# Copies for sums of weight blocks, paced by tiles of the stage that runs beside them, in a decoder block on one core

## The chip, the cores and the metric

The program runs on one core of a Trainium2 chip. The core has TensorE (PE, with its weight loads as PEld), VectorE (DVE), ScalarE (ACT), GpSimd (POOL) and SyncE (SP), which here only issues DMA transfers. The metric is the device time of one execution in microseconds (us), lower being better; the median of three runs counts.

## The reference

One layer of a decoder block on 1024 tokens of width 1024, all in float32:

```python
h = rms_norm(x, norm_mix)
q_flat, kv_flat, g_attn, u_pool, g_merge = split(h @ w_in)
a = nsa_attention(q_flat, kv_flat, g_attn, ...) @ w_branch_attn   # compressed, selected, window branches
b = pool_mixer(u_pool, pool_w, pool_scale) @ w_branch_pool        # trailing means over 2, 4, 8, 16 tokens
ga, gb = split(sigmoid(g_merge))
x = x + (ga * a + gb * b) @ w_out
h = rms_norm(x, norm_mlp)
x = x + square(relu(h @ w_ff1)) @ w_ff2                           # 1024 -> 4096 -> 1024
return rms_norm(x, norm_final)
```

## The kernel before, in words

Every product of float32 matrices is made of three matmuls (`mm3`, L74 to L79): each operand is split into a part rounded to the matmul's type and a rest, and high x high, high x low and low x high are added in PSUM. The split of a weight is made on the fly in `load` (L164 to L183): SP loads 128 x 512 values into `wraw` (four buffers), ScalarE casts them to `whi` (three buffers), and GpSimd, or VectorE where the call says so, subtracts to get `wlo` (three buffers).

The stages, in order of time. First the keys and values of the projection, with `x` loaded and normalised (0 to about 53 us). Then a second block of the projection with 280 columns together with the compression of keys and values (to about 140 us), and two blocks of queries, stored to DRAM as `qd` through two buffers `q` after a rotation on GpSimd (to about 265 us). Their weights stay resident in ten buffers `bhi` and `blo`. Then the pooling branch (`pool_in`, `pool_mix`, to about 345 us) and the gated projection, a loop over eight column blocks `m` of 128 (L480 to L501), which stores the tiles `gb` to DRAM as `gbd`. Then attention (to about 852 us): a written-out interleaving of 32 pairs of heads, 8 blocks of 128 queries by 4 pairs, each pair writing its part of `oT`; between their steps PE gets 128 terms of the other gate's projection, `ga_terms`, stored as `tad`. Then the merge of the branches and the output projection, in two halves of 512 tokens (`ta` and `gb` are loaded back, to about 1003 us), and the feed-forward part.

The feed-forward matrices are multiplied by a scheme of seven block products in place of eight, which needs sums of weight blocks. `weight_sums` (L198 to L216) makes these 32 sums in DRAM, each 1 MB: a copy of one block into `wsw_ff`, issued by SP, and later a DMA from POOL that adds a second block or an earlier sum onto it. The generator is advanced once per `m` of the gated projection and up to 26 times in the attention. Its copies have no input but the weights and write fresh DRAM. The program is scheduled by a framework that sets the order on each engine by its own estimate of when an instruction's inputs are there, so the order in the source isn't that on the engines.

Of the kernel before, what the change touches and what calls it, by code (L numbers as in the profile page):

```python
# [8 lines left out]
F32 = mybir.dt.float32  # L9
# [8 lines left out]
P = 128  # L18
S = 1024
# [3 lines left out]
HALF = 512  # L23
# [26 lines left out]
def build(tc, a, out, dbg=None):  # L50
    nc = tc.nc
# [141 lines left out]
    tad = [[dram.tile([P, HALF], F32, name=f"tad{m}_{h}") for h in range(2)] for m in range(NK)]  # L193


    wsum = {}

    def weight_sums():  # L198
        late = []
        for layer in ("w_ff1", "w_ff2"):  # L200
            for fh in range(2):
                for p in (7, 6, 5, 3):
                    for h in range(2):
                        d = dram.tile([P, 2048], F32, name=f"ws{layer}{fh}{p}{h}")
                        wsum[layer, fh, p, h] = d
                        (m0, k0), (m1, k1) = {7: ((0, 0), (1, 0)), 6: ((1, 1), (0, 0)), 5: ((1, 0), (1, 1)),
                                              3: ((0, 1), (0, 0))}[p]
                        nc.sync.dma_start(d, a[layer][fh, m0, k0, h])
                        prior = {6: 7, 3: 6}.get(p)
                        late.append((d, a[layer][fh, m1, k1, h] if prior is None else wsum[layer, fh, prior, h]))  # L210
                        if len(late) > 1:
                            d_, src = late.pop(0)
                            nc.gpsimd.dma_start(d_, src, accum_op=ADD, max_dma_last_dim=2048)
                        yield
        for d_, src in late:
            nc.gpsimd.dma_start(d_, src, accum_op=ADD, max_dma_last_dim=2048)  # L216

    sums = weight_sums()


# [201 lines left out]
    with ExitStack() as st:  # L422
# [6 lines left out]
        with ExitStack() as st2:  # L429
# [48 lines left out]
                    pool_mix(*prev)  # L478
                prev = cur
            for m in range(NK):  # L480
                next(sums)
                gh, gl = load(cols(a["w_in"], C_GB + m * P, P))
                bh, bl = load(cols(a["w_branch_pool"], m * P, P, 0, 4))
                zz = []
                for hf in range(2):
                    sl = slice(hf * HALF, (hf + 1) * HALF)
                    ps = psF.tile([P, HALF], F32, name="psF")
                    mm3(ps, [(gh[:, k], gl[:, k], XH[k][:, sl], XL[k][:, sl]) for k in range(NK)])
                    z = wg.tile([P, HALF], F32, name="z", bufs=3)
                    nc.vector.tensor_tensor(z, ps, rB[:, sl], op=MUL)  # L490
                    nc.scalar.activation(z, z, AF.Tanh, scale=0.5)
                    zz.append(z)
                if m == 0:
                    pool_mix(*prev)
                for hf in range(2):
                    sl = slice(hf * HALF, (hf + 1) * HALF)
                    ps = psF.tile([P, HALF], F32, name="psF")
                    mm3(ps, [(bh[:, k], bl[:, k], mxh[:, k, sl], mxl[:, k, sl]) for k in range(4)])
                    gb = wg.tile([P, HALF], F32, name="gb", bufs=2)
                    nc.vector.scalar_tensor_tensor(gb, zz[hf], 1.0, ps, op0=ADD, op1=MUL)  # L500
                    nc.sync.dma_start(gbd[m][hf], gb)  # L501


    octx = ExitStack()
    op = pool(octx, "o", side="right")
    oT = op.tile([P, 4, S], F32, name="oT")
    with ExitStack() as st:
# [172 lines left out]
        pairs = [(i, hp) for i in range(NT) for hp in range(NH // 2)]  # L680
        weight = [min(i + 1, 5) + i + 2 for i, _ in pairs]
        total, nterm = sum(weight), 2 * NK * NK
        done, given, summed = 0.0, 0, 0

        def advance(w):
            nonlocal done, given, summed
            done += w
            while summed < 26 * done / total:
                next(sums, None)
                summed += 1  # L690
            while given < nterm and given < nterm * done / total:
                next(fill, None)
                given += 1
# [5 lines left out]
        for n in range(len(pairs) + 1):  # L699
            aseq = []  # L700
            if n < len(pairs):
                i, hp = pairs[n]
# [14 lines left out]
            for fn, slot in bseq or [(None, True)]:  # L717
                if fn is not None:
                    fn()
                if slot:  # L720
# [3 lines left out]
                        ia += 1  # L724
                    advance(bw / nslot)
            assert ia == na
            if n < len(pairs):
                bseq, bw = units_b(u), weight[n]
        for _ in fill:
            pass  # L730
        for _ in sums:
            pass
        sctx.close()
        dump("oT", oT)
    psTctx.close()
# [44 lines left out]
    with ExitStack() as st:  # L780
        wm = pool(st, "wm")
        for hf in range(2):
# [7 lines left out]
            for m in range(NK):  # L790
                wh, wl = load(cols(a["w_branch_attn"], m * P, P, 0, 4), nc.vector)
                ps = bank()
                mm3(ps, [(wh[:, k], wl[:, k], oh[:, k], ol[:, k]) for k in range(4)])
                ta = wm.tile([P, HALF], F32, name="ta", bufs=2)
                gb = wm.tile([P, HALF], F32, name="gb", bufs=1)
                nc.sync.dma_start(ta, tad[m][hf])
                nc.sync.dma_start(gb, gbd[m][hf])
                nc.vector.scalar_tensor_tensor(ta, ta, 1.0, ps, op0=ADD, op1=MUL)
                nc.vector.tensor_tensor(ta, ta, gb, op=ADD)
                mh = wm.tile([P, HALF], F32R, name=f"mh{m}")  # L800
                ml = wm.tile([P, HALF], F32R, name=f"ml{m}")
                nc.scalar.copy(mh, ta)
                sub(nc.vector, ml, ta, mh)
                mg.append((mh, ml))
# [220 lines left out]
```

## Time and profile before

| | |
|---|---|
| median of 3 runs | 1652.23 us (1650.91 to 1655.87) |
| profiled execution | 1656.69 us |
| its span | 1654.9 us, mean granted TensorE clock 0.943 |
| PE busy | 1480.2 us, 89% of the span |
| DVE, ACT, POOL busy | 1001.7, 758.6, 169.1 us |
| moved by DMA | 204.67 MB, mean 124 GB/s |

A busy time is the time in which an engine executes something; issues of DMA transfers and waits aren't in it. The granted clock is a share of TensorE's full speed. The DMA share is the mean busy share of the core's 16 DMA engines as the packets show it, and can pass 1. A wait is put down to the engine or transfer that came last, by line: `POOL wsw_ff L213 <- DMA wsw_ff<-in_w_ff` says that GpSimd waited in front of its DMA at line 213 until a transfer into `wsw_ff` had landed.

### The profile page before, as it was taken

The page shows a single profiled execution, that of the slowest core. Times are in us where ns is not written, and L with a number is a line of the kernel's source. Part 1 is how long each engine was busy: PE and PEld are TensorE (multiplying, and loading weights), DVE is VectorE, ACT ScalarE, POOL GpSimd, SP SyncE. Part 2 cuts the span into 40 slices and gives each one's busy share as a digit, 9 for nine tenths or more (in the row PEclk, how much of TensorE's full clock was granted, in tenths as well). Part 3 has the DMA queues.
Part 4 walks back from the last instruction along what each step waited for, and adds up shares of the span by engine and source line. Part 5 has one row for each costly group of instructions (what it writes and reads, how often), then busy time and mean ns, then how long its engine had stood idle before and what let it go on. Part 6 is the DMA issues. An engine that isn't in the chain of part 4 may idle for free.

```text
span 1654.9 us, 20716 instructions
## 1 busy us (share of the span) xinstructions
PE 1480.2 (89%) x7369; PEld 1222.5 (74%) x7369; DVE 1001.7 (61%) x1928; ACT 758.6 (46%) x1561; POOL 169.1 (10%) x206
## 2 busy tenths in 40 slices
PE   8766554669999999999998989999999999999995
PEld 6755453558877788887876878888888888888874
DVE  5554101331118888887765575766789656669984
ACT  4332110121227877777753344557434453764441
POOL 2111333122220000000001010000000000001020
PEclk9878677789999999999999999999999999999997
DMA  8999999962231110010046533333333333333322
GB/s 304 289 286 222 262 275 280 230 144 83 77 102 46 38 46 21 33 33 26 27 136 214 148 104 107 94 100 97 97 95 97 96 96 96 96 96 97 96 63 102
DMA packets 130137, 204.67 MB, mean 124 GB/s; under 512 B 9840, under 2 KB 62832, under 8 KB 129520
## 3 DMA queue, kind: packets, MB, share of 16 engines
q1 hardware_dynamic: 112992, 169.78, 32.8%
q0 software_dynamic: 16896, 33.56, 11.5%
q8 instruction: 58, 0.95, 0.2%
q14 instruction: 47, 0.39, 0.1%
q10 hardware_dynamic: 144, 0.00, 0.0%
HBM read 186.52 MB, written 83.89 MB: 163 GB/s over the span
## 4 chain that ended last, share of the span: by engine, by line
PE 71%; DMA 3%; DVE 3%; ACT 2%; issue 1%; POOL 0%; POOLq 0%; DVEq 0%; SPq 0%; ACTq 0%
PE psm L79 14%; PE psm L77 14%; PE psm L78 14%; PE oacc L659 5%; PE psT L648 4%; PE psF L79 3%; PE psF L78 3%; PE psF L77 3%; DMA gb<-gbd 3%; PE psS L553 2%; PE psS L554 2%; PE psG L77 2%; PE psG L78 2%; PE psG L79 2%; PE psS L556 1%
## 5 line engine op out<-in xcount | busy, mean ns | idle before, releaser
L78 PE MATMUL psm<-mv,whi 128*128 128x512 f32 x896 | 351.9, 393 | 0.0
L77 PE MATMUL psm<-mv,whi 128*128 128x512 f32 x896 | 351.8, 393 | 0.0
L79 PE MATMUL psm<-mv,wlo 128*128 128x512 f32 x896 | 351.7, 393 | 0.0
L82 DVE TENSOR_TENSOR wlo<-wraw,whi 128x512 fp32r<-128x512 f32 x288 | 197.9, 691 | 109.9 <-ACT whi L858 70.3
L858 ACT CAST whi<-wraw 128x512 fp32r<-128x512 f32 x224 | 138.8, 620 | 247.9 <-PE psm L78 185.9
L78 PEld LDWEIGHTS psm<-mv,whi 128*128 128x128 f32 x896 | 169.0, 189 | 37.0
L77 PEld LDWEIGHTS psm<-mv,whi 128*128 128x128 f32 x896 | 168.9, 189 | 36.9
L79 PEld LDWEIGHTS psm<-mv,wlo 128*128 128x128 f32 x896 | 168.9, 188 | 36.8
L179 ACT CAST whi<-wraw 128x512 fp32r<-128x512 f32 x112 | 69.4, 622 | 175.3 <-PE psF L78 77.0
L79 PE MATMUL psF<-xh,wlo 128*128 128x512 f32 x192 | 79.1, 412 | 50.7 <-POOL wlo L82 50.7
L652 DVE TENSOR_TENSOR pl<-psT,ph 128x512 fp32r<-128x512 f32 (+1 forms) x160 | 101.9, 646 | 31.1 <-ACT ph L651 29.7
L754 POOL TENSOR_TENSOR sqa<-sqa,sq 128x512 f32<-128x512 f32 x24 | 33.1, 1381 | 803.0 <-ACT sq L750 803.0
L651 ACT CAST ph<-psT 128x512 fp32r<-128x512 f32 (+1 forms) x160 | 87.6, 555 | 50.1 <-PE psT L648 48.4
L563 DVE TENSOR_REDUCE nm<-psS 128x1 f32<-128x64 f32 (+8 forms) x192 | 99.6, 539 | 16.4 <-PE psS L556 9.0
L82 POOL TENSOR_TENSOR wlo<-wraw,whi 128x512 fp32r<-128x512 f32 x48 | 64.3, 1350 | 422.5 <-ACT whi L179 299.3
L77 PE MATMUL psF<-bhi,xh 128*128 128x256 f32 (+1 forms) x192 | 63.9, 335 | 40.0 <-ACT q L392 15.1
L79 PEld LDWEIGHTS psF<-xh,wlo 128*128 128x128 f32 x192 | 38.3, 199 | 60.2 <-POOL wlo L82 52.0
L77 PE MATMUL psF<-xh,whi 128*128 128x512 f32 x192 | 78.4, 408 | 2.8 <-ACT q L392 2.8
L78 PE MATMUL psF<-xl,whi 128*128 128x512 f32 x192 | 78.0, 406 | 0.0
L77 PEld LDWEIGHTS psF<-bhi,xh 128*128 128x128 f32 x192 | 43.9, 230 | 42.8 <-ACT q L392 15.4
L564 ACT ACTIVATE pS<-psS,nm 128x64 f32<-128x64 f32 (+8 forms) x128 | 67.9, 532 | 8.3 <-DVE nm L563 7.9
L838 ACT CAST mv<-mt 128x512 fp32r<-128x512 f32 x96 | 59.1, 617 | 20.0 <-DVE mt L836 15.5
(241 smaller groups left out, 3119.1 us busy)
## 6 DMA issues: line engine op xcount, KB each, us to landing
wraw<-wsw_ff SPq DMA_DIRECT2D x128, 256.0 KB, 3.1
wraw<-in_w_ff SPq DMA_DIRECT2D x96, 256.0 KB, 3.1
wsw_ff<-in_w_ff POOLq DMA_DIRECT2D x16, 1024.0 KB, 27.2
wsw_ff<-wsw_ff POOLq DMA_DIRECT2D x16, 1024.0 KB, 18.0
wraw<-in_w_in SPq DMA_DIRECT2D x40, 256.0 KB, 2.9
wraw<-in_w_out SPq DMA_DIRECT2D x32, 256.0 KB, 3.1
xt<-in_x SPq DMA_DIRECT2D x8, 512.0 KB, 5.2
qd<-q SPq DMA_DIRECT2D x16, 256.0 KB, 8.7
```

The source lines that it names most:

```text
L77: nc.tensor.matmul(ps, lhsT=sh, rhs=mh, start=first and i == 0, stop=False, skip_group_check=more)
L78: nc.tensor.matmul(ps, lhsT=sh, rhs=ml, start=False, stop=False, skip_group_check=more)
L79: nc.tensor.matmul(ps, lhsT=sl, rhs=mh, start=False, stop=last and i == n - 1, skip_group_check=more)
L82: eng.tensor_tensor(lo, src, f(hi), op=SUB)
L179: nc.scalar.copy(h, v)
L563: nc.vector.tensor_reduce(nm, v, axis=AX.X if flat else AX.XY, op=MAX, negate=True)
L564: nc.scalar.activation(p if flat else p.rearrange("p (a n) -> p a n", a=2), v, AF.Exp, bias=nm, accum_out=sm)
L648: nc.tensor.transpose(ps[:, j, e], src[e][:, c0:c0 + P], ident)
L651: nc.scalar.copy(ph[:, :n], ps[:, :n])
L652: nc.vector.tensor_tensor(pl[:, :n], ps[:, :n], f(ph[:, :n]), op=SUB)
L659: nc.tensor.matmul(o, lhsT=v, rhs=part[:rows, j], start=gi == 0 and j == 0 and part is ph, stop=2 * gi + j == nb - 1 and part is pl)
L858: nc.scalar.copy(hi, raw)
```

## The change

There are three edits. The copies of the sums are issued by POOL in place of SP, and ahead of each, SP writes four values of a given tile into the first four places of the sum's DRAM tile; the copy overwrites them, and so has to wait until that small write, a marker, has landed. The markers come from the last `gb` of the previous `m` in the gated projection (7 sums), and from the `oT` of the pair two steps back in the attention (at most one sum per pair, 24 or so, the rest behind the last pair). Third, in the merge `ta` gets three buffers in place of two, and `gb` two in place of one.

```diff
--- before.py
+++ after.py
@@ -193,7 +193,8 @@
     tad = [[dram.tile([P, HALF], F32, name=f"tad{m}_{h}") for h in range(2)] for m in range(NK)]
 
 
-    wsum = {}
+
+    wsum, made = {}, []
 
     def weight_sums():
         late = []
@@ -205,7 +206,8 @@
                         wsum[layer, fh, p, h] = d
                         (m0, k0), (m1, k1) = {7: ((0, 0), (1, 0)), 6: ((1, 1), (0, 0)), 5: ((1, 0), (1, 1)),
                                               3: ((0, 1), (0, 0))}[p]
-                        nc.sync.dma_start(d, a[layer][fh, m0, k0, h])
+                        nc.sync.dma_start(d[0:1, 0:4], made.pop())
+                        nc.gpsimd.dma_start(d, a[layer][fh, m0, k0, h])
                         prior = {6: 7, 3: 6}.get(p)
                         late.append((d, a[layer][fh, m1, k1, h] if prior is None else wsum[layer, fh, prior, h]))
                         if len(late) > 1:
@@ -478,7 +480,8 @@
                     pool_mix(*prev)
                 prev = cur
             for m in range(NK):
-                next(sums)
+                if made:
+                    next(sums)
                 gh, gl = load(cols(a["w_in"], C_GB + m * P, P))
                 bh, bl = load(cols(a["w_branch_pool"], m * P, P, 0, 4))
                 zz = []
@@ -499,6 +502,7 @@
                     gb = wg.tile([P, HALF], F32, name="gb", bufs=2)
                     nc.vector.scalar_tensor_tensor(gb, zz[hf], 1.0, ps, op0=ADD, op1=MUL)
                     nc.sync.dma_start(gbd[m][hf], gb)
+                made[:] = [gb[0:1, 0:4]]
 
 
     octx = ExitStack()
@@ -683,11 +687,8 @@
         done, given, summed = 0.0, 0, 0
 
         def advance(w):
-            nonlocal done, given, summed
+            nonlocal done, given
             done += w
-            while summed < 26 * done / total:
-                next(sums, None)
-                summed += 1
             while given < nterm and given < nterm * done / total:
                 next(fill, None)
                 given += 1
@@ -724,12 +725,19 @@
                         ia += 1
                     advance(bw / nslot)
             assert ia == na
+            if n >= 2 and summed < 25 * done / total:
+                i, hp = pairs[n - 2]
+                made[:] = [oT[0:1, hp, i * P:i * P + 4]]
+                next(sums, None)
+                summed += 1
             if n < len(pairs):
                 bseq, bw = units_b(u), weight[n]
         for _ in fill:
             pass
-        for _ in sums:
-            pass
+        while len(wsum) < 32:
+            made[:] = [oT[0:1, 3, S - 4:S]]
+            next(sums)
+        next(sums, None)
         sctx.close()
         dump("oT", oT)
     psTctx.close()
@@ -791,8 +799,8 @@
                 wh, wl = load(cols(a["w_branch_attn"], m * P, P, 0, 4), nc.vector)
                 ps = bank()
                 mm3(ps, [(wh[:, k], wl[:, k], oh[:, k], ol[:, k]) for k in range(4)])
-                ta = wm.tile([P, HALF], F32, name="ta", bufs=2)
-                gb = wm.tile([P, HALF], F32, name="gb", bufs=1)
+                ta = wm.tile([P, HALF], F32, name="ta", bufs=3)
+                gb = wm.tile([P, HALF], F32, name="gb", bufs=2)
                 nc.sync.dma_start(ta, tad[m][hf])
                 nc.sync.dma_start(gb, gbd[m][hf])
                 nc.vector.scalar_tensor_tensor(ta, ta, 1.0, ps, op0=ADD, op1=MUL)
```

On SP's queue, at the end of the first stage and in the compression (`in_w_in` and `in_cmp_k_w` are weights of the projection and the compression, `wsw_ff` are the sums), the order before is:

```order
L178 DMA wraw<-in_w_in 128x280 x4
L208 DMA wsw_ff_2406<-in_w_ff 16x16384
L178 DMA wraw<-in_w_in 128x280 x4
L208 DMA wsw_ff_2526<-in_w_ff 16x16384
L178 DMA wraw<-in_cmp_k_w 128x512 x4
L208 DMA wsw_ff_2635<-in_w_ff 16x16384
L178 DMA wraw<-in_cmp_k_w 128x512
L315 DMA w_746<-in_cmp_k_w 128x2x64
L208 DMA wsw_ff_2744<-in_w_ff 16x16384
```

and in the changed program:

```order
L178 DMA wraw<-in_w_in 128x280 x8
L178 DMA wraw<-in_cmp_k_w 128x512 x7
L317 DMA w_746<-in_cmp_k_w 128x2x64
L317 DMA w_914<-in_cmp_v_w 128x2x64
L178 DMA wraw<-in_cmp_k_w 128x512
L178 DMA wraw<-in_cmp_v_w 128x512 x8
L178 DMA wraw<-in_w_in 128x256 x13
L397 DMA qd_102<-q 128x512
L397 DMA qd_103<-q 128x512
```

The copies are gone from between the loads; the loads of the second block and of the compression stand one behind the other.

On POOL, at the start of the gated projection (the tiles `wlo` are the subtractions, with the semaphores that each waits for; `DMAHW` counts transfers of SP, `DMASW` those of POOL), before, from the last accumulating transfer on:

```order
L216 DMA wsw_ff2131_7549<-wsw_ff2161_6918 512x512 [waits DMAHW1_49,DMASW7_49,DMASW3_49]
L82 TENSOR_TENSOR wlo_2325<-wraw_2323,whi_2324 128x512 [waits DMAHW2_49,PE_49,Activation_49]
L82 TENSOR_TENSOR wlo_2410<-wraw_2408,whi_2409 128x512 [waits DMAHW3_49,PE_49,Activation_49]
L82 TENSOR_TENSOR wlo_2416<-wraw_2414,whi_2415 128x512 [waits DMAHW6_49,PE_49,Activation_49]
L82 TENSOR_TENSOR wlo_2422<-wraw_2420,whi_2421 128x512 [waits DMAHW0_49,PE_49,Activation_49]
L82 TENSOR_TENSOR wlo_2531<-wraw_2529,whi_2530 128x512 [waits DMAHW2_49,PE_49,Activation_49]
```

and now, from the subtraction ahead of the first copy on:

```order
L82 TENSOR_TENSOR wlo_2541<-wraw_2539,whi_2540 128x512 [waits DMAHW4_49,PE_49,Activation_49]
L210 DMA wsw_ff1070_2524<-in_w_ff1 16x16384 [waits DMAHW2_49]
L82 TENSOR_TENSOR wlo_2639<-wraw_2637,whi_2638 128x512 [waits DMAHW5_49,PE_49,Activation_49]
L215 DMA wsw_ff1070_2524<-in_w_ff1 512x512 [waits DMASW0_49]
L82 TENSOR_TENSOR wlo_2645<-wraw_2643,whi_2644 128x512 [waits DMAHW6_49,PE_49,Activation_49]
L82 TENSOR_TENSOR wlo_2651<-wraw_2649,whi_2650 128x512 [waits DMAHW7_49,PE_49,Activation_49]
L210 DMA wsw_ff1071_2633<-in_w_ff1 16x16384 [waits DMAHW0_49]
L82 TENSOR_TENSOR wlo_2749<-wraw_2747,whi_2748 128x512 [waits DMAHW3_49,PE_49,Activation_49]
L215 DMA wsw_ff1071_2633<-in_w_ff1 512x512 [waits DMASW2_49]
```

A copy now stands behind every third subtraction and waits for its marker (`DMAHW`), one subtraction later comes the accumulating transfer, which waits for the copy (`DMASW`), and two subtractions are queued behind it.

On SP, at the end of the attention and the start of the merge, before:

```order
L534 DMA tad_1_141<-z 128x512
L796 DMA ta<-tad_0_126 128x512
L797 DMA gb<-gbd_0_110 128x512
L796 DMA ta<-tad_0_128 128x512
L812 DMA accx<-in_xT 128x512 x6
L178 DMA wraw<-in_w_branch_attn 128x4x128
L797 DMA gb<-gbd_0_112 128x512
L796 DMA ta<-tad_0_130 128x512
L812 DMA accx<-in_xT 128x512
L178 DMA wraw<-in_w_out 128x4x128
```

and now:

```order
L209 DMA wsw_ff_7946<-oT 1x4
L804 DMA ta<-tad_0_126 128x512
L805 DMA gb<-gbd_0_110 128x512
L804 DMA ta<-tad_0_128 128x512
L805 DMA gb<-gbd_0_112 128x512
L804 DMA ta<-tad_0_130 128x512
L820 DMA accx<-in_xT 128x512 x4
L178 DMA wraw<-in_w_branch_attn 128x4x128
L805 DMA gb<-gbd_0_114 128x512
L804 DMA ta<-tad_0_132 128x512
```

The last marker stands ahead of the first load of `ta`; four loads of `accx` come before the next weights in place of six, and two loads of `gb` ahead of them in place of one.

## Rows read from the trace of the kernel before

**Rows 1.** The page's slices, 40 of equal length: DMA busy tenths.

```profile
DMA  8999999962231110010046533333333333333322
```

**Rows 2.** Busy us by stretch: length, PE PEld DVE ACT POOL, clock, DMA share, GB/s.

```profile
53.00:140.00 87.00, 55.95 (x348) 51.96 (x347) 50.74 (x153) 31.71 (x81) 10.85 (x13) 0.81 1.05 286
140.00:265.00 125.00, 77.28 (x456) 70.81 (x455) 18.01 (x79) 22.91 (x52) 42.92 (x97) 0.78 1.05 260
265.00:345.00 80.00, 31.18 (x111) 24.66 (x112) 24.84 (x28) 9.41 (x13) 18.99 (x20) 0.69 1.06 244
...
363.00:487.00 124.00, 123.63 (x544) 101.86 (x543) 22.23 (x33) 25.59 (x41) 29.68 (x23) 1.00 0.27 78
487.00:852.00 365.00, 354.86 (x2296) 288.07 (x2295) 289.86 (x680) 271.58 (x690) 18.16 (x14) 1.00 0.12 37
852.00:932.00 80.00, 74.59 (x309) 58.98 (x310) 42.59 (x67) 28.43 (x49) 8.13 (x6) 0.96 0.65 201
932.00:1003.00 71.00, 65.36 (x291) 54.02 (x290) 45.31 (x77) 28.64 (x48) 8.07 (x6) 0.95 0.46 132
```

**Rows 3.** Waits, 0 to 480 us: us in total, times, longest.

```profile
POOL wsw_ff L213 <- DMA wsw_ff<-in_w_ff: 159.9, 24, 45.2
...
ACT q L392 <- DMA qd<-q: 66.8, 13, 15.7
...
PE psF L79 <- POOL wlo L82: 50.7, 3, 23.8
...
PE psT L360 <- DVE kvA L149: 18.1, 2, 16.5
...
PE psF L77 <- ACT q L392: 17.8, 3, 8.2
...
PE psF L77 <- DVE vst L268: 7.4, 1, 7.4
```

**Rows 4.** DMA issues, whole span: count, KB each, median us to landing.

```profile
wsw_ff<-in_w_ff POOLq DMA_DIRECT2D x16, 1024.0 KB, 27.2
...
qd<-q SPq DMA_DIRECT2D x16, 256.0 KB, 8.7
gbd<-gb SPq DMA_DIRECT2D x16, 256.0 KB, 2.0
...
wsw_ff<-in_w_ff SPq DMA_DIRECT2D x32, 13.7
```

**Rows 5.** Timeline of SP's queue: start us, us, instruction.

```profile
33.31 0.60 SPq L208 DMA_DIRECT2D wsw_ff<-in_w_ff  x1
...
388.97 3.06 SPq L501 DMA_DIRECT2D gbd<-gb  x2
```

**Rows 6.** Timeline of POOL: in brackets idle before, and what ended it.

```profile
41.44 1.16 POOL L213 DMA_DIRECT2D wsw_ff<-in_w_ff  x1 [2.08 <-DMA wsw_ff<-in_w_ff]
...
399.59 1.29 POOL L82 TENSOR_TENSOR wlo<-wraw,whi 128x512 fp32r<-128x512 f32 x1 [6.87 <-ACT whi L179]
402.32 1.29 POOL L82 TENSOR_TENSOR wlo<-wraw,whi 128x512 fp32r<-128x512 f32 x1 [1.43 <-ACT whi L179]
407.75 1.29 POOL L82 TENSOR_TENSOR wlo<-wraw,whi 128x512 fp32r<-128x512 f32 x1 [4.14 <-ACT whi L179]
...
650.50 1.27 POOL L82 TENSOR_TENSOR wlo<-wraw,whi 128x512 fp32r<-128x512 f32 x1 [33.78 <-ACT whi L179]
662.09 1.29 POOL L82 TENSOR_TENSOR wlo<-wraw,whi 128x512 fp32r<-128x512 f32 x1 [10.31 <-ACT whi L179]
```

**Rows 7.** The tile `wsw_ff`, 0 to 365 us: ns min/median/max, first and last start.

```profile
L213 POOL DMA_DIRECT2D wsw_ff<-in_w_ff x16: 1005/1024/1843, 41.4 to 317.9; - x16
```

**Rows 8.** Timeline of VectorE, in the attention.

```profile
838.29 0.75 DVE L620 TENSOR_SCALAR pS<-pS,cc 128x1024 f32<-128x1024 f32 x1
```

**Rows 9.** The chain that ended last, 852 to 1003 us: shares by line.

```profile
by line: DMA gb<-gbd 28.9%; PE psm L79 19.8%; PE psm L77 19.4%; PE psm L78 19.0%; DVE ta L799 5.5%; issue 2.0%; PE psm L136 1.4%; DVE wlo L82 1.4%; DVE accx L815 0.7%; ACT mh L802 0.6%; ACT oh L787 0.4%; SPq L796 0.3%; SPq L534 0.2%; DVE sq
```

**Rows 10.** Waits, 852 to 1003 us.

```profile
DVE ta L799 <- DMA gb<-gbd: 14.0, 14, 4.1
```

## The prediction

> **What bounds the kernel now.** I read the page's slices first. The DMA engines are at nine tenths or more in seven of the first eight of 40 slices and mostly under a half from slice ten on [rows 1]: whatever is wrong is wrong before 345 us. Then the busy times by stage [rows 2]; there the reader should multiply PE's busy time by the granted clock, which gives the matmul work at full clock. From 53 to 345 us that is 55.95 x 0.81 + 77.28 x 0.78 + 31.18 x 0.69 = 45 + 60 + 22 = 127 us of work in 292 us. From 363 to 852 us, the gated projection and the attention, PE is busy 478 of 489 us at clock 1.00 while the DMA share is 0.27 and 0.12. So the front of the program waits, with the DMA share at 1.05; the middle is bound by PE and has DMA time to spare.
>
> The waits of the front say for what [rows 3]. GpSimd stands 159.9 us in front of the accumulating transfers of the weight sums until their copies land. Behind them on its queue are the subtractions that make `wlo`, and PE idles 50.7 us for these. ScalarE stands 66.8 us until stores of `q` land; PE's idle before `psT` (18.1) and `psF` (17.8) hangs on that. That is 87 us of PE idle behind DMA in three rows. What does not hang on DMA is small: 7.4 us for `vst` at the first transition. The transfers [rows 4] show the cause: 32 copies and 32 accumulating transfers of 1 MB each, median 13.7 and 27.2 us to land, and in the same stretch a 256 KB store of `q` takes 8.7 us, where the same size stored in the gated projection (`gbd`) takes 2.0.
>
> **The change part by part.**
>
> *The sums leave the front.* No copy can start before the first `gb` of the gated projection is made; 64 transfers of 1 MB go, out of the 77 MB that the rates of [rows 2] make for 53 to 345 us (the first few lie before it). What then limits each stage? I take the busiest engine plus what it can't overlap. From 53 to 140 us VectorE is busy 50.7 us, more than PE's 45; with the 7.4 us for `vst` and about 3 of start I take 61. From 140 to 265 us it is PE with 60; two changes of the resident weights (a load of about 3 us, then cast and subtraction, some 4 to 5 us each) and a few us in which the two `q` buffers are short make 73. From 265 to 345 VectorE has 25 and PE 22, in turn in places: 32. Together 166 us, of which 39 are not matmul work. Idle also costs clock: before, 164 us busy held 127 of work, so 37 us were lost to the clock beside 128 us of idle, 0.29 for each. 39 x 0.29 = 11, so 177 in place of 292: **115 us less**. Bounds: 165 less if PE never paused (292 - 127), and 75 less if the chains through ScalarE, VectorE and GpSimd leave a little less than the 87 us that the three rows name.
>
> *The gated projection gets 7 sums.* Each iteration is 72 matmuls; 544 took 123.63 us [rows 2], 0.227 each, so 16.3 us. GpSimd now has, after the third subtraction, the copy; after the next subtraction the accumulating transfer, which waits for that copy; behind it the subtraction for the second `w_in` tile, and for that PE waits. The clock of one iteration [rows 5, 6]: the stores of `gb` are issued by 392.0, the marker store lands 2.0 later (the `gbd` row), so the copy is issued at 394.1. The first subtraction runs at 399.6, the second would at 402.3. The third, at 407.75, stands with its cast just behind the matmuls that end the iteration, so the next iteration starts at about 407.1 and comes to the second tile 12 matmuls later, at 409.8. Taking off 1.3 for the subtraction and 1.0 for the issue, the copy may take 13.4 us to land before PE waits. The copy at 33.31 us, issued when little else was under way, let its follower go at 41.44: 8.1 us. The load per iteration is 2 MB of sums beside 1.3 MB, 200 GB/s where the front moved 244 to 286. I take 8.1, so **nothing**; the far end is 7 x (27.2 - 13.4) = 97 us, at the landing time of the accumulating transfers. It can't gain: PE is busy 123.6 of 124 us.
>
> *The attention gets 25.* PE waits on GpSimd for 16 `wlo` tiles. The second tile of a block is subtracted at 650.5, the block before ends at about 662 (the next subtraction, 662.09), and PE reaches the second half four terms later; 128 terms in 365 us are 2.85 each, so at about 673: 21 us of slack. GpSimd can be held by a copy that waits for its marker, at most one pair of heads (365 / 32 = 11.4 us), and by one landing (8.1): 19.5. **2 us more** for the odd case; bounds 0 and, with the landing at 27.2 on the eight second tiles, 8 x (11.4 + 27.2 - 21) = 141. On SP's queue `qi`, `tad` and weight loads now stand behind marker stores that wait for `oT`; `qi` is asked for one group (two pairs, 23 us) ahead, so that is cover enough. The 32 markers are 32 more issues for SP, an engine that mostly waits.
>
> A rule speaks against this part. The issues of accumulating transfers took 1.005 to 1.843 us on GpSimd in the front [rows 7], with VectorE busy 94 of 292 us; in the attention it is busy 290 of 365, with scalings of `pS` of 0.75 us [rows 8]. The Trainium skill, page "SBUF — State Buffer", section "SBUF: two separate sides", says that while VectorE runs a mode that takes both SBUF ports, GpSimd is locked out and can't write the descriptors of a DMA that it issues. No row of this case has the two beside each other. By that rule a copy and its follower would start up to 2 x 0.75 us later, 21.0 instead of 19.5 against a slack of 21: an estimate from that page and these rows, by which the sum stays and the third rival below comes nearer.
>
> *The merge.* `ta` gets three buffers, `gb` two, so a load of `gb` no longer waits for the addition before it. The chain runs through those loads for 28.9% of 852 to 1003 us, but VectorE waits only 14.0 us for them [rows 9, 10], and PE has 74.59 x 0.96 + 65.36 x 0.95 = 134 us of work in 151. At most 17 us are to be had; some of that is the start and the norm in the middle, I take 8. Against it, the markers of the last two sums are made by the last two pairs of heads, so a copy and two accumulating transfers fall into the first 20 us of the merge, where DMA is already at 0.65: 3.1 MB at 201 GB/s are 16 us if all of it is in the way. Loads of `accx` there are early; I take 4. **4 us less**, between 17 less and 16 more.
>
> The feed-forward part is untouched: its sums are made long before it reads them, as now.
>
> **Sum.** 1656.7 (profiled execution: span 1654.9 and 1.8 around it) - 115 + 0 + 2 - 4 = 1539.7. The median of the runs is 4.5 below the profiled one, so **1535 us**.
>
> **Rivals.**
> 1. *The front is bound by its own chains.* For: VectorE at 51 of 87 us in its first third, two `q` buffers, weights resident in ten buffers. Against: the three rows of DMA waits. With 75 less: 1575.
> 2. *The sums hold up `wlo`.* The wait of GpSimd for its copies moves along with them and PE waits for `wlo` in the gated projection. For: this is the very wait that cost 50.7 us before, and copies took 13.7 in the median, just over 13.4. Against: that was at a DMA share above 1. Landing halfway between 13.7 and 27.2, at 20.4: 7 x 7 = 49 us, 1584.
> 3. *Slower: GpSimd's queue becomes the bound in the attention.* Each of the 16 subtractions stands behind a sum, and if the slack were used up each would cost PE a landing of 13.7 us: 219 us, 1535 + 219 = 1754. It decides from 117 / 16 = 7.3 us per tile, which means GpSimd held for 28 us before each. Against: 19.5 is what I find, and half of the tiles (the first of a block) have some 45 us of slack (16 terms).
> 4. *Nothing changes*: the marker doesn't delay the copy, or the time goes back in full: 1652. The order has the copy waiting on the marker's semaphore.
>
> **How the numbers follow.** Forecast 0.70, with 1512 to 1560 as its own range. Rival 1 has 0.12, since its chains show in the trace but hidden behind the waits. Rival 2 has 0.13, since 8.1 and 13.7 stand on either side of 13.4 and the higher comes from a fuller DMA. Rival 3 has 0.04, since it needs both the slack gone and a third more. Rival 4 has 0.01. Low end: about 28 us more in front and merge than I take, 1508; high end 1580, which takes in rival 1 and the near half of rival 2. About 0.3% is what a measurement can tell from no change: faster 0.95, same 0.01, slower 0.04.
>
> **What would show it.** In the profile after: DMA under a half between 60 us and the start of the gated projection; the first `gb` about 115 us earlier; the stretch of the front with VectorE or PE busy over 75%; stores of `q` landing in under 4 us; GpSimd's waits for copies long, but PE's waits for `wlo` near zero; the DMA share in the attention at 0.4 to 0.7 with the same 365 us; PE idle in the merge smaller in its second half than in its first. Wrong: PE idle for `wlo` in whole tens of us, or a first stretch that still has a third of its time idle with DMA quiet.

## The result, and the profile after

The changed kernel takes **1511.18 us** (median of 4 runs, 1510.19 to 1513.18) against 1652.59 us for the kernel before, run beside it: a ratio of 0.9144, 95% interval 0.9126 to 0.9161. The forecast was 1535, with 1508 to 1580 as its range; the time lies 1 us under the narrower 1512 to 1560 that the prediction gave a chance of 0.70. The profiled execution took 1510.39 us (span 1508.6, mean granted clock 0.981, PE busy 96% of the span).

Five landmarks cut both spans into the same pieces: the first and the last store of `gb`, the last store of `ta`'s source (`tad`), the first load of `w_ff`, and the end. All kernels of this study are in one table, by the starts of these instructions in one profiled execution of each, in us. Executions of the kernel before range over up to 12 us (1647.67 to 1659.51 in 13 runs), so a difference of a few us between fronts with unpaced sums is not to be read; the kernels with paced sums stay within some 5 us. One execution of `before, no GpSimd work` took 2084.99 us at a granted clock of 0.647, where its others had 0.952 to 0.957, and is left out of its time below.

| kernel | to first `gbd` | gated projection | attention | merge | rest | span |
|---|---|---|---|---|---|---|
| before | 372.6 | 117.0 | 362.3 | 136.7 | 666.3 | 1654.9 |
| after | 224.1 | 117.0 | 367.4 | 135.4 | 664.7 | 1508.6 |
| pacing only | 224.4 | 117.0 | 367.1 | 142.6 | 666.3 | 1517.4 |
| buffers only | 362.5 | 117.0 | 361.0 | 129.9 | 666.9 | 1637.3 |
| copies on SP, paced | 223.9 | 118.2 | 366.7 | 138.9 | 666.3 | 1514.0 |
| no sums | 222.3 | 117.1 | 361.9 | 128.3 | 664.6 | 1494.2 |
| before, no GpSimd work | 333.4 | 117.1 | 360.3 | 138.6 | 666.7 | 1616.1 |
| before, plain copies | 320.4 | 117.0 | 363.9 | 135.3 | 666.4 | 1603.0 |
| before, both | 288.9 | 117.0 | 358.9 | 136.9 | 665.2 | 1566.9 |
| after, no GpSimd work | 221.7 | 117.0 | 361.1 | 136.9 | 664.7 | 1501.4 |
| after, unpaced traffic | 233.6 | 172.9 | 362.7 | 137.4 | 664.8 | 1571.4 |
| two sums per block | 223.4 | 143.3 | 371.7 | 128.5 | 666.2 | 1533.1 |
| last sum left to attention | 222.9 | 117.0 | 361.3 | 146.8 | 664.7 | 1512.7 |
| four sums early | 227.6 | 115.1 | 362.3 | 128.2 | 664.7 | 1497.9 |

So the change gained 148.5 us in the front, nothing in the gated projection, lost 5.1 in the attention, and gained 1.3 in the merge and 1.6 behind it. The page's slices after answer to [rows 1]; PE's row is put with DMA's:

```profile
PE   8999999997999999999899999999999999999995
...
DMA  8234217875668777867944333333332223332312
```

The first slices are no longer full; the DMA share lies in slices 7 to 20 instead, which are the gated projection, the attention and the start of the merge. The windows after, with the columns of [rows 2], on the stages' new places:

```profile
53.00:140.00 87.00, 77.82 (x576) 73.40 (x576) 63.25 (x216) 44.09 (x115) 15.36 (x44) 0.96 0.30 91
140.00:163.00 23.00, 23.00 (x182) 22.32 (x181) 1.47 (x4) 6.59 (x11) 15.90 (x45) 1.00 0.40 129
163.00:197.00 34.00, 33.82 (x150) 27.63 (x148) 22.89 (x25) 9.11 (x13) 11.07 (x9) 1.00 0.20 53
...
222.00:341.00 119.00, 118.29 (x522) 97.60 (x521) 20.62 (x30) 22.54 (x36) 38.46 (x36) 1.00 0.78 194
341.00:709.00 368.00, 354.68 (x2288) 288.27 (x2288) 288.62 (x680) 271.73 (x690) 55.22 (x62) 0.99 0.72 174
709.00:789.00 80.00, 75.05 (x307) 59.65 (x308) 42.14 (x67) 28.40 (x49) 9.31 (x8) 0.96 0.79 240
789.00:858.00 69.00, 65.86 (x292) 54.50 (x290) 44.73 (x78) 29.09 (x48) 8.69 (x6) 0.95 0.42 127
```

From 53 to 197 us PE is busy 134.6 of 144 us at a clock of 0.96 to 1.00. The same work took 53 to 345 us before: 197 is 345 less the 148.5 gained. Look at the first row: 576 matmuls in the 87 us that held 348 in [rows 2], and VectorE's 63 us lie beside them. The waits from 53 to 345 us (us in total, times, longest) show what PE still waits for there; three of the ten rows, which come to about 10 us in all:

```profile
PE psF L77 <- DVE vst L270: 3.3, 1, 3.3
PE psT L362 <- DVE kvA L149: 2.7, 6, 1.0
PE psF L77 <- ACT bhi L179: 1.0, 1, 1.0
```

The rows of [rows 3] for `wlo`, and for `psF` behind `q`, are gone. What GpSimd and ScalarE wait for, from 0 to 480 us:

```profile
POOL wsw_ff L215 <- DMA wsw_ff<-in_w_ff: 35.3, 10, 7.6
...
POOL wsw_ff L210 <- DMA wsw_ff<-gb: 28.6, 7, 5.8
...
ACT q L394 <- DMA qd<-q: 5.1, 3, 3.3
```

GpSimd's waits for copies go on, but up to 480 us no single one is longer than 7.6 us (9.6 in the whole span), where the longest was 45.2; ScalarE's wait for stores of `q` fell from 66.8 to 5.1.

### The profile page after: what moved, and what is told of

It is laid out like the page before. It is cut to its first block, busy times and chain, and to the rows that moved or that the text cites. A ratio compares the mean times of both kernels' runs of the same rounds, so it can differ in the third digit from the quotient of the medians.

```text
span 1508.6 us, 20793 instructions
## 1 busy us (share of the span) xinstructions
PE 1451.2 (96%) x7369; PEld 1199.6 (80%) x7369; DVE 1001.3 (66%) x1928; ACT 760.6 (50%) x1561; POOL 187.6 (12%) x238
## 4 chain that ended last, share of the span: by engine, by line
PE 84%; DVE 6%; DMA 5%; ACT 3%; issue 1%; POOL 1%; SPq 0%; POOLq 0%; DVEq 0%; ACTq 0%
PE psm L78 16%; PE psm L77 16%; PE psm L79 16%; PE oacc L663 5%; PE psF L78 5%; PE psF L79 5%; PE psF L77 5%; PE psT L652 4%; PE psS L557 3%; PE psS L558 2%; PE psG L77 2%; PE psG L78 2%; PE psG L79 2%; DMA xt<-in_x 1%; PE psS L560 1%
## 5 line engine op out<-in xcount | busy, mean ns | idle before, releaser
L82 POOL TENSOR_TENSOR wlo<-wraw,whi 128x512 fp32r<-128x512 f32 x48 | 65.6, 1368 | 108.1 <-ACT whi L179 88.2
L78 PE MATMUL psF<-xl,whi 128*128 128x512 f32 x192 | 74.7, 389 | 0.0
L77 PE MATMUL psF<-xh,whi 128*128 128x512 f32 x192 | 74.7, 389 | 0.0
L79 PE MATMUL psF<-xh,wlo 128*128 128x512 f32 x192 | 74.7, 389 | 0.0
L82 DVE TENSOR_TENSOR mv<-mt,mv 128x512 fp32r<-128x512 f32 x96 | 67.3, 708 | 1.1 <-ACT mv L846 0.6
L663 PE MATMUL oacc<-ph,vst 128*128 128x256 f32 x264 | 64.1, 318 | 1.2 <-ACT ph L655 0.9
L652 PE MATMUL psT<-cf,pS 128*128 128x128 f32 x352 | 60.4, 276 | 2.8 <-DVE pS L624 2.6
```

What stands on the lines that cost most here:

```text
L77: nc.tensor.matmul(ps, lhsT=sh, rhs=mh, start=first and i == 0, stop=False, skip_group_check=more)
L78: nc.tensor.matmul(ps, lhsT=sh, rhs=ml, start=False, stop=False, skip_group_check=more)
L79: nc.tensor.matmul(ps, lhsT=sl, rhs=mh, start=False, stop=last and i == n - 1, skip_group_check=more)
L82: eng.tensor_tensor(lo, src, f(hi), op=SUB)
L652: nc.tensor.transpose(ps[:, j, e], src[e][:, c0:c0 + P], ident)
L663: nc.tensor.matmul(o, lhsT=v, rhs=part[:rows, j], start=gi == 0 and j == 0 and part is ph, stop=2 * gi + j == nb - 1 and part is pl)
```

## Why the front was slow: experiments on the cause

That the sums left the front explains the gain only as a whole. Two things left with them: GpSimd's queue, in which subtractions stood behind waiting transfers, and the traffic. The two were undone one at a time, from the kernel before and from the kernel after. A third thing, the copies' place between the loads on SP's queue, was not undone by itself.

**GpSimd's work on VectorE, sums as before** (1611.25 us, the median of three executions; ratio to before 0.9733, 0.9705 to 0.9761):

```diff
-            sub(lo_eng or nc.gpsimd, l, v, h)
+            sub(lo_eng or nc.vector, l, v, h)
-                rope(nc.gpsimd, q.rearrange("p h e d -> p (h e) d"), 8, cosT[:, t], sinT[:, t], wkA)
+                rope(nc.vector, q.rearrange("p h e d -> p (h e) d"), 8, cosT[:, t], sinT[:, t], wkA)
...
```

> The kernel before, with the work of GpSimd in the front (subtractions for wlo, the rotation of q, the rests of w2 and of the pooling weights, two memsets) on VectorE, so that nothing stands behind GpSimd's accumulating transfers; the sums keep their early, unpaced start. Theory A (the DMA engines are full, and loads and stores land late whatever the queues do): the front stays at 372 us to the first store of gb, give or take 30, and the time at 1620 to 1660. Theory B (GpSimd's queue in its order: it stands 160 us for copies, and wlo and q stand behind it): most of the 148 us come back, 1520 to 1570.

Nothing stands behind GpSimd's queue now, and it waits longer there than before (0 to 340 us):

```profile
POOL wsw_ff L213 <- DMA wsw_ff<-in_w_ff: 232.7, 23, 41.2
```

Yet only 39.2 of the 148.5 us come back. Theory A, though nearer, had asked for a front within 30 us of 372 and falls short too: the queue is a real part of the loss, and about a quarter of it. The time, 1611, lies under theory A's 1620 and far above theory B's range.

**Traffic that nobody waits for, added to the kernel after** (1573.87 us, 0.9508, 0.949 to 0.9527):

```diff
+            nc.sync.dma_start(d, a["w_ff1"][n % 2, n // 2 % 2, n // 4 % 2, n // 8 % 2])
...
+                for _ in range(8):
+                    next(extra, None)
```

> The kernel after, with 64 copies of 1 MB from DRAM to DRAM that nobody waits for and that aren't paced, issued by SP in the front as the copies were before; nothing of them stands on GpSimd's queue. Theory A (full DMA engines): the first store of gb goes from 224 back to 320 to 380 us, the stores of q land in 8 us or more, and the time is 1600 to 1660. Theory B (GpSimd's queue): the first store of gb stays within 20 us of 224, and the time is under 1535.

Neither. The first `gbd` came only 9.5 us later, as theory B had it, but the time is 63 us longer: 3 of the 64 copies were issued before 53 us, 36 between 53 and 234 us, and 25 in the gated projection, which took 56 us more. The windows of this kernel say why the two places differ:

```profile
53.00:140.00 87.00, 77.05 (x569) 72.71 (x570) 64.33 (x219) 44.00 (x113) 15.12 (x43) 0.96 0.80 271
140.00:234.00 94.00, 88.05 (x452) 74.62 (x452) 39.41 (x47) 25.08 (x38) 32.38 (x58) 0.96 0.90 309
234.00:410.00 176.00, 130.37 (x528) 103.71 (x528) 20.20 (x30) 22.89 (x37) 39.05 (x36) 0.87 0.95 291
```

At a DMA share of 0.80 and 0.90 PE loses almost nothing; with the paced sums on top, at 0.95, it loses a quarter of the stretch. And 271 to 309 GB/s pass here at a lower share than the 286 to 244 GB/s of [rows 2] at 1.05. The test was not as heavy as the traffic it was to stand for, since it had no accumulating transfers. The trace gives their price. DMA queues from 53 to 234 us (packets, MB, share of the 16 engines' time), before:

```profile
q0 software_dynamic: 9504, 18.88, 58.6%
q1 hardware_dynamic: 10598, 29.71, 47.3%
```

GpSimd's queue (q0) carries only accumulating transfers: 0.586 x 181 / 18.88 = 5.6 us of all engines per MB; SP's queue takes 0.473 x 181 / 29.71 = 2.9. So the next kernel has the same queue, order and waits, with plain copies.

**Plain copies in place of the accumulating transfers, in the kernel before** (1602.60 us, 0.968, 0.9649 to 0.971):

```diff
-                            nc.gpsimd.dma_start(d_, src, accum_op=ADD, max_dma_last_dim=2048)
+                            nc.gpsimd.dma_start(d_, src, max_dma_last_dim=2048)
```

> The kernel before, with the 32 accumulating transfers turned into plain copies of the same shape on GpSimd's queue, which overwrite the first block; each waits for the same copy as before, and the order on every engine is the same. The sums are left out by it. So it has GpSimd's queue standing as before, and cheaper transfers: between 53 and 234 us of the kernel before, GpSimd's queue moved 18.88 MB in 58.6% of the engines' time and SP's 29.71 MB in 47.3%, twice as much time for each MB. Theory A (the additions fill the DMA engines, and everything else lands late): the first store of gb at 235 to 290 us, and the time 1520 to 1570. Theory B (GpSimd's queue in its order, whatever the transfers cost): the first store of gb stays above 330, and the time above 1610.

```profile
q1 hardware_dynamic: 11653, 36.84, 58.5%
q0 software_dynamic: 5979, 23.06, 38.8%
```

Over the same 181 us GpSimd's queue now takes 0.388 x 181 / 23.06 = 3.0 us per MB: the addition, and not the queue, nearly doubles the price. It also nearly doubles the packets, from 259 to 503 per MB, and a packet takes an engine much the same time with and without it (0.18 and 0.19 us); so whether the adding or the smaller packets cost the time isn't parted here. The first `gbd` comes at 320.4, 52.2 us earlier, and between the two theories. Of PE's waits from 53 to 340 us of this kernel, the largest is still the one behind GpSimd's order:

```profile
PE psF L79 <- POOL wlo L82: 36.0, 2, 26.1
```

**Both edits together** (1575.38 us, 0.9529, 0.9507 to 0.9551):

> The same plain copies in place of the accumulating transfers (the sums are left out by it), and the work of GpSimd in the front on VectorE, so that nothing stands behind its queue. With the kernel before, the one with GpSimd's work moved, and the one with plain copies it makes a table of two by two. If the front is lost to these two things and no third, the first store of gb comes at 225 to 255 us, and the time is 1500 to 1540. If it stays above 280, the unpaced copies by themselves, or VectorE's greater load, cost as much.

The first `gbd` at 288.9: neither edit hides the other, and a third part is left. Its windows have PE idle with the DMA engines nearly full, where the kernel with added traffic had 0.80 and 0.90:

```profile
53.00:140.00 87.00, 62.61 (x375) 58.53 (x376) 51.07 (x157) 31.09 (x82) 7.51 (x12) 0.79 0.99 343
140.00:250.00 110.00, 83.14 (x507) 74.63 (x506) 50.48 (x183) 27.55 (x55) 8.20 (x13) 0.87 0.96 325
```

It takes the next kernel to say whether VectorE's greater load has a part in it.

**The kernel after, GpSimd's work on VectorE** (1504.12 us, 0.9094, 0.9076 to 0.9112; the edit is that of the first experiment):

> The kernel after, with the work of GpSimd in the front on VectorE: what that move costs by itself, where no sum stands in the front. Theory (VectorE has the room): the first store of gb at 222 to 236 us, and the time 1508 to 1525. Rival (VectorE becomes the bound of the front): above 250, and then as much of the time of the kernel before with GpSimd's work moved isn't DMA.

VectorE has the room: the first `gbd` comes at 221.7 with no sums in the front, and the time is even under the range. So the table of two by two closes. From the kernel before to this one the front becomes 150.9 us shorter: 39.2 by taking the work from behind GpSimd's queue (372.6 to 333.4), 44.5 by making the second transfers plain (333.4 to 288.9), and 67.2 by removing what is left, 64 MB of plain unpaced copies (288.9 to 221.7). In the other order the first two are 52.2 and 31.5. The traffic as a whole is thus 112 to 119 of the 151 us. These are single executions: by the medians of the whole time the first three steps are 43, 36 and 71 us, so each is good to some 7 us. The last step also takes the copies from between the loads on SP's queue, and its 67 us are not parted into the two. In the kernel with added traffic 36 copies between the loads of the front cost 9.5 us, at a DMA share of 0.80 to 0.90; so the place on the queue costs little by itself there, while at 0.96 to 0.99 nothing was tried that parts them. That the added traffic cost 65.4 us in all is a near figure by chance: 55.9 of it fell in another stage, beside paced sums.

**Copies back on SP, with their markers** (1513.98 us, 0.9148, 0.913 to 0.9166) asks whether the move to GpSimd's queue was needed:

```diff
-                        nc.gpsimd.dma_start(d, a[layer][fh, m0, k0, h])
+                        nc.sync.dma_start(d, a[layer][fh, m0, k0, h])
```

> The kernel after, with the copies issued by SP again and the markers kept: pacing without the move to GpSimd's queue. Theory (the pacing alone makes the gain): within 10 us of the kernel after, 1508 to 1521, the few us for SP's queue standing about 2 us for each marker with loads behind it. Rival (the copies had to leave SP's queue): the loads of weights stand behind copies that wait for oT, PE waits for whi in the gated projection and the attention, 1530 or more.

It wasn't: the front is the same to 0.2 us, and the ratio lies within the interval of the change. The pacing makes the gain of the front without the move. Whether the move without the markers would have made some of it was not tried.

## What the sums still cost: experiments on the rest

**No sums at all** (1496.13 us, 0.9039, 0.9021 to 0.9058):

```diff
-                        nc.sync.dma_start(d[0:1, 0:4], made.pop())
-                        nc.gpsimd.dma_start(d, a[layer][fh, m0, k0, h])
+                        wsum[layer, fh, p, h] = a[layer][fh, m0, k0, h]
...
```

> The kernel after without any of the 32 sums: no marker, no copy, no accumulating transfer; the feed-forward part multiplies plain blocks of the weights in their place, with as many loads and matmuls. It gives the floor that pacing can reach. Theory: what the sums still cost is the late load of qi at the start of the attention (4.6 us) and 2 to 4 us in the merge, so 1502 to 1506. Rival 1: they are wholly hidden, 1509 to 1512. Rival 2: they cost GpSimd's issues and DMA time all through the gated projection and the attention, under 1495.

The floor lies 15 us below the change, between the theory's 1502 and rival 2's 1495: the sums cost more than the theory had. (It leaves the sums out of the product, so it is a floor for the time only.) The table puts it in two places: 5.5 us in the attention and 7.1 in the merge, beside 1.8 in the front. The attention's is at its very start. Its first PE row with a wait, and two windows around it, in the kernel after:

```profile
347.85 1.12 PE L549 MATMUL psT<-cf,qi 128*128 128x128 f32 x4 [4.60 <-DMA qi<-qd]
```

```profile
336.00:344.00 8.00, 6.41 (x27) 4.63 (x26) 1.38 (x2) 0.87 (x2) 3.63 (x3) 1.00 0.84 149
344.00:352.00 8.00, 4.15 (x17) 3.73 (x17) 1.15 (x3) 0.78 (x2) 0.00 (x0) 0.59 0.79 244
```

PE waits 4.60 us for `qi`, whose loads SP issues at 340.32 and 341.47 us, while the seventh sum's accumulating transfer, issued at 336.86, may still be under way. Behind that idle time PE's granted clock is 0.59 in the mean, near the lower of its two levels (1.2 of 2.4 GHz), so the wait costs clock beside its 4.60 us; the attention is 5.1 us longer in all than before. What holds `qi` up was the next test's question.

**The last column block of the gated projection without a sum** (1516.51 us, 0.9175, 0.9153 to 0.9197):

```diff
-                if made:
+                if made and m < NK - 1:
```

> The kernel after without the sum of the last column block of the gated projection, which then has 6 sums in place of 7; the attention takes the one more at its own pace. Theory (the loads of qi at the start of the attention land late because that sum is under way): the wait of 4.6 us in front of psT goes, 1505 to 1508. Rival (qi is late for another reason, such as its place on SP's queue): 1510 to 1513.

The cause was right and the time wrong. The wait for `qi` is gone and the attention takes 361.3 us, 6.1 less. But one more sum is left over for the end, and the merge takes 11.4 more. GpSimd's queue at that place (start us, us), the last pair of heads ending at 701:

```profile
697.51 1.01 POOL L215 DMA_DIRECT2D wsw_ff<-in_w_ff  x1 [5.76 <-DMA wsw_ff<-in_w_ff]
707.47 1.02 POOL L210 DMA_DIRECT2D wsw_ff<-in_w_ff  x2 [8.96 <-DMA wsw_ff<-oT]
714.51 1.07 POOL L215 DMA_DIRECT2D wsw_ff<-wsw_ff  x1 [6.02 <-DMA wsw_ff<-in_w_ff]
717.09 1.04 POOL L218 DMA_DIRECT2D wsw_ff<-wsw_ff  x1 [1.52 <-DMA wsw_ff<-in_w_ff]
```

```profile
701.00:740.00 39.00, 24.71 (x87) 18.91 (x88) 15.16 (x25) 8.53 (x16) 3.13 (x4) 0.81 1.06 296
```

Two copies and two additions fall among the merge's first loads; PE is busy 25 of 39 us. In the kernel after one copy and one addition fall behind the attention's end, and PE is busy 34 of 40. The second late sum cost the merge more here (11.4 us) than the first (5.5, the buffers' test below).

**Four sums early, and the last one before the merge** (1498.07 us, 0.9061, 0.9039 to 0.9084):

```diff
+                made[:] = [pl[0:1, 16:20]]
+                next(sums)
...
+                if made and m < NK - 1:
...
+            if n >= 2 and summed < 22 and summed < 26 * done / total:
```

> The kernel after without the sum of the last column block of the gated projection, with 4 sums paced by pl in the pooling branch, and at most 22 in the attention, so that the last one is made before the merge begins. Theory (what the sums still cost is the late qi, 4.6 us, and their collision with the loads of the merge, 2 to 4 us): 1501 to 1506. Rival 1 (the 8 MB more in the pooling branch stand on GpSimd's queue in front of wlo): the first store of gb comes 5 to 20 us later, 1510 to 1525. Rival 2 (the merge loses nothing by the sums): as without the last sum of the gated projection alone.

As the theory had it, though 3 us under its range: the attention at 362.3, the merge at 128.2, and 3.5 us lost in the pooling branch. It beats both the kernel before and the kernel after, and stands 2 us above the floor without sums, with overlapping intervals.

**Pacing without the buffers** (1519.14 us, 0.9192, 0.9171 to 0.9214) and **the buffers without the pacing** (1644.86 us, 0.995, 0.9929 to 0.997) part the merge:

```diff
-                ta = wm.tile([P, HALF], F32, name="ta", bufs=3)
-                gb = wm.tile([P, HALF], F32, name="gb", bufs=2)
+                ta = wm.tile([P, HALF], F32, name="ta", bufs=2)
+                gb = wm.tile([P, HALF], F32, name="gb", bufs=1)
```

> The kernel after, with the buffers of the merge as before (two of ta, one of gb). Theory of the prediction (the buffers gain 8 us and the last sums lose 4): 5 to 9 us slower than the kernel after, 1516 to 1520. Rival (the loads of gb were hidden beside PE, and the buffers gain nothing): within 2 us of the kernel after.

> The kernel before, with three buffers of ta and two of gb in the merge, the sums as before. In this kernel no sum runs beside the merge. Theory of the prediction: 8 us faster than before, 1643 to 1646. Rival (the loads were hidden beside PE): 0 to 2 us faster, 1650 to 1653.

The buffers gain 7.2 us of the merge with the sums beside it (142.6 to 135.4), and 6.8 without (136.7 to 129.9), as the theory had it to a microsecond or so; the medians say 8 and 6.5. The sums cost the merge 5.9 us with the old buffers and 5.5 with the new ones (7.1 against the kernel without any sums). (The second kernel's front came at 362.5, which its edit doesn't touch; the 13 runs of the kernel before beside it spread over 12 us.)

**Two sums per block of the gated projection** (1534.27 us, 0.9274, 0.9256 to 0.9293):

```diff
-                if made:
+                while made:
                     next(sums)
...
-                made[:] = [gb[0:1, 0:4]]
+                made[:] = [gb[0:1, 0:4], gb[0:1, 4:8]]
```

> The kernel after with two sums in each column block of the gated projection, 14 in place of 7, and 18 in the attention. Each block then asks for 4 MB of sums beside 1.3 MB of its own in 16.3 us, 325 GB/s. Theory of the prediction (a copy that takes over 13.4 us to land makes PE wait for wlo): the first to the last store of gb take 135 to 180 us in place of 117, and the time is 1525 to 1570. Rival (the queue carries it, and fewer sums are left for the end of the attention and the merge): 117 to 122 us, and 1505 to 1513.

The gated projection takes 143.3 us, and PE's waits between 220 and 400 us are:

```profile
PE psF L79 <- POOL wlo L82: 16.1, 5, 6.4
PE psT L549 <- DMA qi<-qd: 10.8, 1, 10.8
```

The wait that rival 2 feared is there, at twice the load, and so is the late `qi`, now 10.8 us. Most of the 26.3 us that the gated projection lost are the 16.1 in front of `psF`; the clock was granted at 0.94 from 220 to 345 us, where the kernel after has 1.00 in this stage. The fewer sums at the end give 6.9 us back in the merge.

## Why the prediction was right in kind, and 24 us long

- **The front, −115 foreseen, −148.5 measured.** The mechanism was right; the term was mis-sized. The step that failed is "Together 166 us, of which 39 are not matmul work", and the clock term of 11 that hangs on it. Most of the 39 are allowances for what each stage can't overlap (10 us, 13 and 7), beside a first stage that goes at VectorE's pace. But the stages overlap once nothing holds them: the first store of `qd` moved from 165.9 to 116.1 us, so the query matmuls ran beside VectorE's work for the compression. Measured are 144 us in place of 177: 131.5 us of matmul work (77.82 x 0.96 + 23.00 + 33.82, where the same working gave 127 before), 9.4 us of idle time in place of 39, and 3 us lost to the clock in place of 11. The bound of 165, PE never pausing, was 17 us off, the value taken 33. Nor did the 87 us of the three rows of DMA waits bound the gain: all of PE's waits from 53 to 365 us came to 127 us before, and those of 12.3 and 11.2 us for casts of weights (`whi`, `bhi`), which wait for loads, went as well.
- **The total missed by 24 us, less than the front, by luck.** The attention and the merge together came out 5.8 us worse than taken, and the 4.5 us that the sum takes off for the median against the profiled execution were not there in the changed kernel (1511.18 and 1510.39); both made up for a part of the front's 33.5.
- **"The transfers [rows 4] show the cause"** held, but said nothing of why. Of 150.9 us, GpSimd's order is 31 to 39, the price of the additions 45 to 52, and the plain traffic 67, with the copies' place on SP's queue in it; each is good to some 7 us.
- **The gated projection, 0 foreseen, 0 measured.** GpSimd's timeline shows the landing that this hung on:

```profile
246.63 0.55 POOL L210 DMA_DIRECT2D wsw_ff<-in_w_ff  x1 [2.42 <-DMA wsw_ff<-gb]
...
252.72 1.02 POOL L215 DMA_DIRECT2D wsw_ff<-in_w_ff  x1 [0.34 <-DMA wsw_ff<-in_w_ff]
```

  From the copy's issue to its follower's are 6.1 us (5.2 to 6.9 over the seven), where 8.1 was taken and 13.4 allowed. Rival 2 (1584) did not come at this load; its wait came at twice the load.
- **The attention, +2 foreseen, +5.1 measured**, and for another reason: not a `wlo` behind GpSimd's queue, which no PE wait there names, but a late `qi`. "`qi` is asked for one group (two pairs, 23 us) ahead, so that is cover enough" failed for the first group, which has no group before it. The DMA share of the attention, 0.72, lies just over the 0.4 to 0.7 that was to show it: 24 additions take the engines 2.7 us more each than copies would, 0.18 of the stretch.
- **The rule on VectorE's ports** (the Trainium skill, page "SBUF — State Buffer", section "SBUF: two separate sides") didn't show as longer issues in this kernel. The transfers on GpSimd's queue in the attention (ns min/median/max, first and last start):

```profile
L210 POOL DMA_DIRECT2D wsw_ff<-in_w_ff x24: 514/517/905, 363.2 to 698.5; - x24
L215 POOL DMA_DIRECT2D wsw_ff<-wsw_ff x12: 993/1018/1032, 368.4 to 704.0; - x12
L215 POOL DMA_DIRECT2D wsw_ff<-in_w_ff x12: 1005/1016/1032, 383.4 to 687.6; - x12
```

  With VectorE busy 289 of 368 us none of the accumulating ones took over 1.032 us; in the front, with VectorE less busy, the longest had 1.843 [rows 7]. In the kernel after with GpSimd's work on VectorE single ones reach 1.402 us in the attention, at a median of 1.018 or less, and no run says whether that is the rule. Rival 3 did not come either way: no wait of PE in the attention names GpSimd.
- **The merge, −4 foreseen, −1.3 measured**: 8 gained and 4 lost were 7 and 6. The waits for `gb` fell from 14.0 [rows 10] to 4.3, and those for `ta` took part of their place. VectorE's waits from 708 to 850 us:

```profile
DVE ta L806 <- DMA ta<-tad: 7.2, 3, 3.3
DVE ta L807 <- DMA gb<-gbd: 4.3, 3, 3.0
```

- **Rival 1**, a front bound by its own chains (1575), is the one that the first window after refutes: the chains were there, beside PE.

## What to carry to other kernels

Where stages can overlap, the time of a stretch freed from a wait can come nearer to the work of its busiest engine over the whole stretch (131.5 of 144 us here) than to a sum over stages with an allowance for waits in each (177). Traffic that nobody needs soon belongs behind a marker from a stretch that is bound by compute; count it in the DMA engines' time rather than in bytes, and end it before the next stage's first loads, which have no cover. When a step is moved out of a queue, test the queue and the traffic apart: here GpSimd's queue was about a quarter of what the front lost, and the traffic with its place on SP's queue the rest.

## What was not expected of the hardware

An accumulating DMA took the 16 engines 5.6 us per MB, a plain one 2.9 to 3.0, in step with its packets per MB (503 and 259 on GpSimd's queue); in the attention of the kernel after, where GpSimd's queue carries as many of the one as of the other, the mixture is 0.594 x 364 / 49.80 = 4.3:

```profile
q0 software_dynamic: 13172, 49.80, 59.4%
```

By these prices the 64 transfers of the sums are worth 32 x (2.9 + 5.6) = 272 us of all 16 engines, nearly the whole of the front's 292.

GpSimd's subtraction takes twice as long as VectorE's on tiles of the same shape, by the page of the kernel after:

```profile
L82 DVE TENSOR_TENSOR wlo<-wraw,whi 128x512 fp32r<-128x512 f32 x288 | 198.8, 694 | 98.8 <-ACT whi L866 70.2
...
L82 POOL TENSOR_TENSOR wlo<-wraw,whi 128x512 fp32r<-128x512 f32 x48 | 65.6, 1368 | 108.1 <-ACT whi L179 88.2
```

The Trainium skill, page "GPSIMD Engine Reference", section "4.1 Engine selection", puts additions of two operands on GpSimd at some 2x VectorE's time, and the trace agrees for subtractions: 1368 to 694 ns. What wasn't expected is that a VectorE busy for 66% of the span gains by it. Moving GpSimd's subtractions and rotations there was meant to show only what that move costs, and made the kernel after faster, 0.9094 against 0.9144 of the time before, with intervals apart. By the table 2.4 us of it are in the front and 6.3 in the attention, whose wait for `qi` fell to 2.7 us; why that load lands sooner there stays open. This edit and the four early sums were not tried together.
